# Two order edges in the weight feed of a transformer block: accumulating transfers in source order, copies of sums beside the casts

## The chip, the cores and the metric

The kernel runs on one core of a Trainium2 chip. The metric is device time in microseconds of one execution; a smaller number is better. The kernel before the change was timed three times: 3212.99 us in the median, from 3210.16 to 3214.57. One further execution was recorded by the hardware profiler; it took 3207.22 us, of which 3205.1 us lie between its first and its last instruction (the span).

Engines by the names of the profile: PE is TensorE (matmuls), PEld its weight loads, DVE is VectorE, ACT is ScalarE, POOL is GpSimd, SP is SyncE, which only issues transfers here.

## The reference

Two blocks run one after the other on 512 tokens of width 1024, all in float32. The first is an attention and gated-linear-attention block with a convolutional feed-forward part. The second has four layers; each layer is a mixer and then a multilayer perceptron, and only the perceptrons matter for this change:

```
def _sqrelu_mlp(h, w1, w2):
    return jnp.square(jax.nn.relu(h @ w1)) @ w2
...
    for i in range(DEPTH_2):                       # 4 layers
        ...
        x = x + mix
        x = x + _sqrelu_mlp(_rmsnorm(x, norm_mlp_g[i]), mlp_w1[i], mlp_w2[i])
```

`w1` is 1024 x 4096 and `w2` is 4096 x 1024.

## The kernel before

Activations lie with channels on the 128 partitions and the 512 tokens along the free dimension. Full float32 accuracy is had from three matmuls in a rounded format: each operand is split into a high part (a rounding cast) and a low part (the operand minus its high part), and high x high, high x low and low x high are summed in PSUM. So each weight panel that comes from memory goes through a cast on ScalarE (`split`, line 273, tile `whi`) and a subtraction on VectorE (line 279, tile `wlo`) before TensorE can use it.

A perceptron (`mlp`) runs in four quarters of the 4096 hidden channels. In each quarter the first product (`w1`) takes eight panels of 1024 columns, 192 matmuls of 512 tokens at lines 196 to 198. VectorE scales the result into `H` (line 1171), ScalarE squares it (line 1172), and `quad` forms seven sums and differences of its quadrants and splits them into `hh` and `hl`. The second product (`w2`) is done by a 2 x 2 block scheme with seven products in place of eight: `pair` (line 308) handles two output tiles at a time, four pairs to a quarter, and each of the seven products of a pair is 12 matmuls of 256 tokens at line 327. So the second stage of a quarter has 4 x 7 x 12 = 336 matmuls, and there are 16 such stages in the four perceptrons. Three PSUM banks serve a pair. Most products accumulate on a bank whose partial sum VectorE must first have added to, or subtracted from, the residual `x` (line 1182, `put`), so a later product on the same bank waits for that instruction.

The seven weight operands of a pair are not all plain pieces of `w2`. With a11, a12, a21, a22 as the quadrants, the feed (class `Feed`) makes sums in SBUF with transfers that add to what lies there:

- `raw` holds a11 and a12 and is loaded by SP.
- `s1` = a21 + a22 and `s3` = a11 + a21: SP loads the first term (line 107), and an adding transfer on GpSimd's queue brings the second (line 104).
- `s2` = s1 + a11 and `s4` = s2 + a12: ScalarE copies the older sum into a new tile (line 112), and an adding transfer brings the other term. So each of these copies waits until the adding transfer of the older sum has landed.
- `a22` is loaded by SP.

Each of these steps has a lead: how many half panels ahead of its pair it stands in the source. A half panel is one `split` of 512 columns; two of them fill one `whi` and one `wlo` tile, of which there are three each (`hl_bufs`). The table in the code:

```
    LEAD = {"raw": 4, "s1": 17, "s1+": 14, "s2": 8, "s3": 9, "s3+": 6, "s4": 2, "a22": 3}
```

The order of the source is not the order on the engines. A scheduler places each engine's instructions by its own estimate of when their inputs are there, and only a dependence keeps two instructions in order. `after(first, then)` (class `K`) states such a dependence without a semaphore: the second instruction must stand behind the first on their engine. Before the change nothing of the kind ties the copies of line 112 to the casts of line 273, or one adding transfer of line 104 to another. Each engine takes its instructions in the order in which they stand.

Of the kernel before, what the change touches and what calls it, by code (L numbers as in the profile page):

```python
# [11 lines left out]
ALU = mybir.AluOpType  # L12
# [45 lines left out]
class Feed:  # L58
# [9 lines left out]
    def __init__(self, k, pool, items):  # L68
        self.k, self.pool = k, pool
        self.acts, self.src = [], []  # L70
        self.n, self.at, self.last = 0, 0, 0
        self.tiles, self.got = {}, []
        for i, it in enumerate(items):
            n = len(self.src)
            (self.panel if it[0] == "panel" else self.pair)(i, n, *it)
        self.acts.sort(key=lambda a: a[0])
        self.acts.reverse()
# [16 lines left out]
    def pair(self, i, n, kind, a, b):  # L94

        k, nc = self.k, self.k.nc
        a11, a12, a21, a22 = a[:, :512], a[:, 512:], b[:, :512], b[:, 512:]

        def tile(tag):
            t = self.tiles[i, tag] = self.pool.tile([P, 512], F32, tag=tag, name=k.nm(tag), bufs=self.BUFS[tag])  # L100
            return t

        def add(t, x):
            nc.gpsimd.dma_start(t, x, accum_op=ALU.add)  # L104

        def two(tag, x, y):
            self.act(n, tag, lambda: nc.sync.dma_start(tile(tag), x))
            self.act(n, tag + "+", lambda: add(self.tiles[i, tag], y))

        def more(tag, old, y):  # L110
            t = tile(tag)
            nc.scalar.copy(t, self.tiles[i, old])  # L112
            add(t, y)

        order = self.ORDER[kind]
        where = {"1": ("raw", 0), "2": ("raw", 512), "6": ("s2", 0), "5": ("s1", 0), "7": ("s3", 0), "3": ("s4", 0),
                 "4": ("a22", 0)}
        self.raw(n, i, a)
        two("s1", a21, a22)
        self.act(n, "s2", lambda: more("s2", "s1", a11))  # L120
        two("s3", a11, a21)
        self.act(n, "s4", lambda: more("s4", "s2", a12))
        self.act(n, "a22", lambda: nc.sync.dma_start(tile("a22"), a22))
        self.src += [(i, *where[p]) for p in order]

    def pump(self):
        k = self.k
        while True:
            while self.acts and self.acts[-1][0] <= self.n:
                self.acts.pop()[1]()  # L130
            if self.n == len(self.src) or self.n // 2 - k.hl_bufs >= self.at // 2:
                return
            if self.n % 2 == 0:
                self.pairs = [k.wp.tile([P, PANEL], F32R, tag=t, name=k.nm(t), bufs=k.hl_bufs) for t in ("whi", "wlo")]
            i, tag, c = self.src[self.n]
            h = slice(512 * (self.n % 2), 512 * (self.n % 2) + 512)
            hi, lo = [t[:, h] for t in self.pairs]
            k.split(hi, lo, self.tiles[i, tag][:, c:c + 512])
            self.got.append((hi, lo))
            self.n += 1  # L140

# [8 lines left out]
class K:  # L150
# [119 lines left out]
    def split(self, hi, lo, src, hi_eng="act", lo_eng="dve"):  # L270
        nc = self.nc
        if hi_eng == "act":
            nc.scalar.copy(hi, src)  # L273
        elif hi_eng == "dve":
            nc.vector.tensor_copy(hi, src)
        else:
            nc.gpsimd.tensor_copy(hi, src)
        e = nc.vector if lo_eng == "dve" else nc.gpsimd
        e.tensor_tensor(lo, src, hi.bitcast(F32), ALU.subtract)  # L279

    def sq_add(self, acc, k, last, src, pool, n, scale=1.0, eng=None, apart=False):

        nc = self.nc
        if k == 0:
            nc.scalar.activation(acc, src, AF.Square, scale=scale)
            return
        s = pool.tile([P, n], F32, tag="sq", name=self.nm("sq"), bufs=2)
        nc.scalar.activation(s, src, AF.Square, scale=scale)  # L288
        if k == last and apart:
            return s  # L290
        (nc.vector if k == last else eng or nc.gpsimd).tensor_tensor(acc, acc, s, ALU.add)  # L291
# [1496 lines left out]
```

## Time and profile before

| what | value |
|---|---|
| three timed runs, median (lowest to highest) | 3212.99 us (3210.16 to 3214.57) |
| profiled execution | 3207.22 us |
| its span | 3205.1 us |
| PE busy in the span | 3029.7 us, 95% |
| DVE busy | 2156.5 us, 67% |
| ACT busy | 1488.9 us, 46% |
| POOL busy | 508.7 us, 16% |
| mean granted TensorE clock | 0.974 of full speed |

"Busy" is the time in which at least one instruction of an engine runs. A matmul's end is modelled and matmuls overlap, so the distance between two starts tells the pace better than the duration of one. The waits of an engine are idle stretches before an instruction, put down to what ended last among the things it waited for. The granted clock is the share of TensorE's full speed that the chip allowed; 1.00 is 2.4 GHz and 0.50 is 1.2 GHz.

### The profile page before, as it was taken

Reading aid. Unit: us, or ns where it says so; the run is one execution under the profiler, and the core shown is the slowest. Engines: PE = TensorE matmul, PEld = TensorE weight load, DVE = VectorE, ACT = ScalarE, POOL = GpSimd, SP = SyncE. Lnnn points to the kernel's source line nnn. Section 1 sums busy time; section 2 is a strip of 40 time slices with the busy share of each in tenths; the row PEclk is TensorE's granted clock in tenths of the full one; section 3 lists DMA queues with packets and bytes.
Section 4 is the critical chain, followed back from the end, with each engine's and each line's share of the span. In section 5 each row is a group of like instructions: output and inputs, shape, how many; then the busy total and the mean of one; then the engine's idle time right before and its main releaser. Section 6 shows DMA issues by size and latency. Waiting matters only on the chain.

```text
span 3205.1 us, 42688 instructions
## 1 busy us (share of the span) xinstructions
PE 3029.7 (95%) x16044; PEld 2596.4 (81%) x16044; DVE 2156.5 (67%) x3596; ACT 1488.9 (46%) x2429; POOL 508.7 (16%) x453
## 2 busy tenths in 40 slices
PE   7999999899999998999999999999999999999998
PEld 4877778688887778888887888888888887788887
DVE  7858885599836856666655666754666688665666
ACT  5436644333334744444444444522544457554444
POOL 3103211100012121111102111101211121121111
PEclk8999999899999999999999999999999999999999
DMA  5661234333333346555425666432655644265663
GB/s 195 204 222 52 90 111 154 139 101 97 96 97 109 106 131 161 143 145 142 120 86 143 150 158 155 106 99 99 160 145 150 158 106 139 86 169 141 151 158 86
DMA packets 164271, 421.09 MB, mean 131 GB/s; under 512 B 18240, under 2 KB 24768, under 8 KB 163040
## 3 DMA queue, kind: packets, MB, share of 16 engines
q1 hardware_dynamic: 118000, 334.91, 32.2%
q0 software_dynamic: 36864, 67.13, 13.3%
q10 hardware_dynamic: 9200, 16.32, 1.5%
q8 instruction: 126, 2.06, 0.3%
q14 instruction: 81, 0.66, 0.1%
HBM read 398.10 MB, written 13.63 MB: 128 GB/s over the span
## 4 chain that ended last, share of the span: by engine, by line
PE 59%; DVE 11%; DMA 11%; issue 4%; ACT 4%; POOL 1%; SPq 0%; POOLq 0%; DVEq 0%; ACTq 0%
PE ps L196 15%; PE ps L198 15%; PE ps L197 15%; PE ps L327 10%; DMA s<-in_w 10%; DVE wlo L279 3%; DVE wlo L182 1%; DVE xc L1257 1%; ACT s L112 1%; DVE hl L279 1%; DVE x L1182 1%; ACT whi L273 1%; ACT hh L273 1%; PE po L217 1%; DVE H L1171 0%
## 5 line engine op out<-in xcount | busy, mean ns | idle before, releaser
L196 PE MATMUL ps<-xh,whi 128*128 128x512 f32 x2224 | 872.5, 394 | 10.4 <-ACT xh L501 6.3
L198 PE MATMUL ps<-xh,wlo 128*128 128x512 f32 x2224 | 872.7, 393 | 6.1 <-DVE wlo L182 4.6
L197 PE MATMUL ps<-xl,whi 128*128 128x512 f32 x2224 | 871.5, 392 | 2.8 <-DVE xl L506 2.8
L327 PE MATMUL ps<-hh,whi 128*128 128x256 f32 x1792 | 525.3, 295 | 89.0 <-DVE x L1182 74.2
L327 PE MATMUL ps<-hl,whi 128*128 128x256 f32 x1792 | 521.9, 292 | 2.2 <-DVE hl L279 1.5
L180 ACT CAST whi<-wraw 128x1024 fp32r<-128x1024 f32 (+2 forms) x267 | 265.1, 995 | 552.0 <-PE ps L197 394.0
L327 PE MATMUL ps<-hh,wlo 128*128 128x256 f32 x1792 | 516.6, 290 | 0.0
L198 PEld LDWEIGHTS ps<-xh,wlo 128*128 128x128 f32 x2224 | 420.2, 189 | 98.3 <-DVE wlo L182 7.9
L196 PEld LDWEIGHTS ps<-xh,whi 128*128 128x128 f32 x2224 | 420.6, 189 | 97.7 <-ACT xh L501 6.5
L197 PEld LDWEIGHTS ps<-xl,whi 128*128 128x128 f32 x2224 | 420.4, 189 | 88.9 <-DVE xl L506 3.5
L327 PEld LDWEIGHTS ps<-hh,whi 128*128 128x128 f32 x1792 | 356.4, 200 | 101.0 <-ACT whi L273 70.7
L182 DVE TENSOR_TENSOR wlo<-wraw,whi 128x1024 fp32r<-128x1024 f32 (+2 forms) x257 | 300.0, 1167 | 189.2 <-ACT whi L180 183.4
L104 POOL DMA_DIRECT2D s<-in_w x256 | 224.8, 997 | 1162.7 <-DMA s<-in_w 748.5
L273 ACT CAST whi<-wraw 128x512 fp32r<-128x512 f32 (+2 forms) x400 | 229.9, 612 | 296.4 <-PE ps L197 203.7
L327 PEld LDWEIGHTS ps<-hl,whi 128*128 128x128 f32 x1792 | 357.9, 200 | 5.7 <-DVE hl L279 4.9
L327 PEld LDWEIGHTS ps<-hh,wlo 128*128 128x128 f32 x1792 | 356.7, 200 | 0.0
L279 DVE TENSOR_TENSOR wlo<-wraw,whi 128x512 fp32r<-128x512 f32 (+2 forms) x400 | 266.5, 696 | 39.4 <-ACT whi L273 26.2
L1182 DVE TENSOR_TENSOR x<-x,ps 128x256 f32<-128x256 f32 x448 | 182.6, 418 | 142.0 <-PE ps L327 138.4
L273 ACT CAST whi<-s 128x512 fp32r<-128x512 f32 x256 | 150.5, 618 | 139.0 <-PE ps L327 110.7
L1171 DVE SCALAR_TENSOR_TENSOR H<-ps,rb 128x512 f32<-128x512 f32 x128 | 88.0, 690 | 155.3 <-PE ps L198 152.5
L291 POOL TENSOR_TENSOR acc_x<-acc_x,sq 128x512 f32<-128x512 f32 x54 | 80.4, 1490 | 670.0 <-ACT sq L288 669.5
L112 ACT COPY s<-s 128x512 f32<-128x512 f32 x128 | 79.4, 620 | 221.1 <-DMA s<-in_w 170.7
(418 smaller groups left out, 4526.9 us busy)
## 6 DMA issues: line engine op xcount, KB each, us to landing
wraw<-in_w SPq DMA_DIRECT2D x192, 512.0 KB, 4.0
s<-in_w POOLq DMA_DIRECT2D x256, 256.0 KB, 5.3
s<-in_w SPq DMA_DIRECT2D x128, 256.0 KB, 3.9
wraw<-in_w_up SPq DMA_DIRECT2D x44, 512.0 KB, 3.4
wraw<-in_a_w_in SPq DMA_DIRECT2D x40, 512.0 KB, 3.5
wraw<-in_w_ada SPq DMA_DIRECT2D x32, 512.0 KB, 4.3
a<-in_w SPq DMA_DIRECT2D x64, 256.0 KB, 3.7
wraw<-in_w_in SPq DMA_DIRECT2D x29, 512.0 KB, 3.8
```

The lines of the kernel that those rows point to most:

```text
L104: nc.gpsimd.dma_start(t, x, accum_op=ALU.add)
L112: nc.scalar.copy(t, self.tiles[i, old])
L180: nc.scalar.copy(hi[:, :n], raw[:, :n])
L182: e.tensor_tensor(lo[:, :n], raw[:, :n], hi[:, :n].bitcast(F32), ALU.subtract)
L196: mm(out, wh, xh, start=start, stop=False)
L197: mm(out, wh, xl, start=False, stop=False)
L198: mm(out, wl, xh, start=False, stop=stop)
L273: nc.scalar.copy(hi, src)
L279: e.tensor_tensor(lo, src, hi.bitcast(F32), ALU.subtract)
L327: mm = lambda *o, **kw: self.nc.tensor.matmul(*o, skip_group_check=not start, **kw)
L1171: nc.vector.scalar_tensor_tensor(h, ps, 0.0, self.rb, ALU.max, ALU.mult)
L1182: nc.vector.tensor_tensor(x[:, n, :], x[:, n, :], ps, ALU.add if sign > 0 else ALU.subtract)
```

## The change

Two order edges are added, both without a semaphore. In `add`, each adding transfer of a feed is tied behind the one issued before it in the source, so that GpSimd's queue holds them in the order of the source. In `more`, each copy of a sum on ScalarE is tied behind the high-part cast that precedes it in the source; `split` now returns that cast so that it can be named. No instruction is added or taken away on any engine.

```diff
@@ class Feed, __init__
+        self.added, self.cast = None, None
@@ pair
         def add(t, x):
-            nc.gpsimd.dma_start(t, x, accum_op=ALU.add)
+            d = nc.gpsimd.dma_start(t, x, accum_op=ALU.add)
+            if self.added is not None:
+                k.after(self.added, d)
+            self.added = d
...
         def more(tag, old, y):
             t = tile(tag)
-            nc.scalar.copy(t, self.tiles[i, old])
+            c = nc.scalar.copy(t, self.tiles[i, old])
+            if self.cast is not None:
+                k.after(self.cast, c)
             add(t, y)
@@ pump
-            k.split(hi, lo, self.tiles[i, tag][:, c:c + 512])
+            self.cast = k.split(hi, lo, self.tiles[i, tag][:, c:c + 512])
@@ split
-            nc.scalar.copy(hi, src)
+            i = nc.scalar.copy(hi, src)
...
         e.tensor_tensor(lo, src, hi.bitcast(F32), ALU.subtract)
+        return i
```

Lines behind the edits have moved: 104 is now 105, 112 is 116, 273 and 279 are 279 and 285, 1172 is 1179, 1182 is 1189.

The first place is ScalarE in the second stage of the second quarter of the first perceptron, around its third pair of output tiles. `whi1668` to `whi1685` are the high parts in the order in which TensorE uses them; `s21670` is the tile `s2` number 1670, and so on. `s21717` and `s41735` are sums of the next quarter. Before:

```order
L273 CAST whi1668_10718<-s41649_10569 128x512
L273 CAST whi1668_10718<-a221644_10527 128x512
L112 COPY s41679_10826<-s21670_10722 128x512
L273 CAST whi1671_10753<-wraw1659_10648 128x512 x2
L273 CAST whi1673_10786<-s21651_10576 128x512
L273 CAST whi1673_10786<-s11622_10387 128x512
L112 COPY s21717_11124<-s11696_10967 128x512
L273 CAST whi1677_10822<-s31650_10572 128x512
L273 CAST whi1677_10822<-s41663_10684 128x512
L112 COPY s41735_11259<-s21717_11124 128x512
L273 CAST whi1683_10860<-a221662_10680 128x512
```

The same stretch with the change:

```order
L279 CAST whi1668_10718<-s41649_10569 128x512
L116 COPY s21670_10722<-s11645_10529 128x512
L279 CAST whi1668_10718<-a221644_10527 128x512
L279 CAST whi1671_10753<-wraw1659_10648 128x512 x2
L279 CAST whi1673_10786<-s21651_10576 128x512
L279 CAST whi1673_10786<-s11622_10387 128x512
L279 CAST whi1677_10822<-s31650_10572 128x512
L116 COPY s41679_10826<-s21670_10722 128x512
L279 CAST whi1677_10822<-s41663_10684 128x512
L279 CAST whi1683_10860<-a221662_10680 128x512
```

The two copies for the next quarter have left this stage (they now stand in the first stage of the next quarter, among the casts of `w1`), and the copies of the fourth pair's own sums (`s21670`, `s41679`) stand later, each between the two casts of one panel.

The second place is GpSimd's queue in the same stage, with the adding transfers alone. Before:

```order
L104 DMA s41649_10569<-in_w2 128x512
L104 DMA s11645_10529<-in_w2 128x512
L104 DMA s21651_10576<-in_w2 128x512
L104 DMA s41663_10684<-in_w2 128x512
L104 DMA s31650_10572<-in_w2 128x512
L104 DMA s21670_10722<-in_w2 128x512
L104 DMA s11696_10967<-in_w2 128x512
L104 DMA s41679_10826<-in_w2 128x512
L104 DMA s31664_10687<-in_w2 128x512
L104 DMA s21717_11124<-in_w2 128x512
```

With the change:

```order
L105 DMA s41649_10569<-in_w2 128x512
L105 DMA s21651_10576<-in_w2 128x512
L105 DMA s11645_10529<-in_w2 128x512
L105 DMA s31650_10572<-in_w2 128x512
L105 DMA s41663_10684<-in_w2 128x512
L105 DMA s21670_10722<-in_w2 128x512
L105 DMA s31664_10687<-in_w2 128x512
L105 DMA s41679_10826<-in_w2 128x512
L105 DMA s11696_10967<-in_w2 128x512
L105 DMA s21717_11124<-in_w2 128x512
```

The transfer of `s11696`, which belongs to the next quarter, now stands behind the two of the fourth pair, and that of `s11645` behind that of `s21651`, which needs a copy first.

The third place is VectorE around the third pair, where the low parts (`wlo`) and the additions to the residual (`x`) share the engine. Before:

```order
L279 TENSOR_TENSOR wlo1678_10823<-s31650_10572,whi1677_10822 128x512
L279 TENSOR_TENSOR wlo1678_10823<-s41663_10684,whi1677_10822 128x512
L1182 TENSOR_TENSOR x_4888<-x_4888,ps1680_10831 128x256
L1182 TENSOR_TENSOR x_4888<-x_4888,ps1681_10832 128x256
L279 TENSOR_TENSOR wlo1684_10861<-a221662_10680,whi1683_10860 128x512
```

With the change:

```order
L285 TENSOR_TENSOR wlo1678_10823<-s31650_10572,whi1677_10822 128x512
L1189 TENSOR_TENSOR x_4888<-x_4888,ps1680_10831 128x256
L285 TENSOR_TENSOR wlo1678_10823<-s41663_10684,whi1677_10822 128x512
L1189 TENSOR_TENSOR x_4888<-x_4888,ps1681_10832 128x256
L285 TENSOR_TENSOR wlo1684_10861<-a221662_10680,whi1683_10860 128x512
```

The addition from `ps1680` now stands ahead of the second low part, whose cast comes after a copy on ScalarE. The other stages change in the same way, and SyncE's order does not change at all. In the last quarter of a perceptron no next quarter exists, so only the copies of its own pairs move there.

## Rows read from the trace of the kernel before

**Rows 1.** The page: busy time, then the chain that ended last by line.
```profile
PE 3029.7 (95%) x16044; PEld 2596.4 (81%) x16044; DVE 2156.5 (67%) x3596; ACT 1488.9 (46%) x2429; POOL 508.7 (16%) x453
...
PE ps L196 15%; PE ps L198 15%; PE ps L197 15%; PE ps L327 10%; DMA s<-in_w 10%; DVE wlo L279 3%; DVE wlo L182 1%; DVE xc L1257 1%; ACT s L112 1%; DVE hl L279 1%; DVE x L1182 1%; ACT whi L273 1%; ACT hh L273 1%; PE po L217 1%; DVE H L1171 0%
```

**Rows 2.** Waits of TensorE: who waited for whom, total us, times, longest.
```profile
PE ps L327 <- DVE x L1182: 74.2, 42, 5.6
PE ps L327 <- ACT hh L273: 14.7, 4, 4.5
```

**Rows 3.** Windows of line 327, quarters one to three: stretch, length, PE, PEld, clock, DMA.
```profile
1332.60:1381.00 48.40, 43.63 (x336) 42.72 (x335) 0.93 0.77 171
...
sum 608.20, PE 528.08 PEld 515.91; mean PE 44.01 PEld 42.99
```

**Rows 4.** Windows of the four last quarters, all engines: PE, PEld, DVE, ACT, POOL.
```profile
1517.60:1563.10 45.50, 42.08 (x338) 40.83 (x337) 39.09 (x65) 26.54 (x45) 12.23 (x10) 1.00 0.45 105
...
sum 179.00, PE 167.68 PEld 162.98 DVE 149.59 ACT 100.57 POOL 47.85; mean PE 41.92 PEld 40.74 DVE 37.40 ACT 25.14 POOL 11.96
```

**Rows 5.** Windows, the first stage (w1) of the second quarter, all engines.
```profile
1289.30:1332.50 43.20, 43.20 (x192) 35.78 (x191) 27.02 (x51) 20.86 (x38) 1.73 (x2) 1.00 0.43 123
```

**Rows 6.** Timeline of TensorE, two starts that are twelve matmuls apart: start, duration.
```profile
1376.04 0.28 PE L327 MATMUL ps<-hh,wlo 128*128 128x256 f32 x1
...
1377.48 0.28 PE L327 MATMUL ps<-hh,wlo 128*128 128x256 f32 x1
```

**Rows 7.** Timeline of ScalarE, second quarter, second stage: start, duration, [idle before].
```profile
1337.17 0.83 ACT L273 CAST hh<-qt 128x768 fp32r<-128x768 f32 x1 [1.09 <-DVE qt L303]
...
1345.07 0.62 ACT L273 CAST whi<-s 128x512 fp32r<-128x512 f32 x1 [1.55 <-PE ps L327]
1345.60 0.62 ACT L273 CAST whi<-a 128x512 fp32r<-128x512 f32 x1
...
1350.83 1.14 ACT L273 CAST whi<-s 128x512 fp32r<-128x512 f32 x2 [1.49 <-PE ps L327]
...
1353.71 1.14 ACT L273 CAST whi<-s 128x512 fp32r<-128x512 f32 x2 [0.33 <-PE ps L327]
1361.19 0.62 ACT L112 COPY s<-s 128x512 f32<-128x512 f32 x1 [6.34 <-DMA s<-in_w]
```

**Rows 8.** Timeline of VectorE, the same stretch.
```profile
1362.36 0.69 DVE L279 TENSOR_TENSOR wlo<-a,whi 128x512 fp32r<-128x512 f32 x1 [5.22 <-ACT whi L273]
...
1363.57 0.74 DVE L1182 TENSOR_TENSOR x<-x,ps 128x256 f32<-128x256 f32 x2
```

**Rows 9.** Timeline of TensorE, the same stretch.
```profile
1364.13 0.55 PE L327 MATMUL ps<-hh,whi 128*128 128x256 f32 x1 [4.58 <-DVE x L1182]
```

**Rows 10.** Windows, the stretch behind that wait, all engines.
```profile
1363.60:1369.00 5.40, 4.87 (x23) 4.90 (x24) 2.34 (x6) 0.90 (x2) 1.13 (x2) 0.50 0.90 183
```

**Rows 11.** Timeline of GpSimd: the adding transfers of `s11645` and `s21717`.
```profile
1327.08 0.86 POOL L104 DMA_DIRECT2D s<-in_w  x1 [40.51 <-DMA s<-in_w]
...
1353.69 0.86 POOL L104 DMA_DIRECT2D s<-in_w  x1 [2.55 <-ACT s L112]
```

**Rows 12.** Landing times of the adding transfers: whole run, then issues 1348.4 to 1352.
```profile
DMA to landing us min/median/max: 4.1/5.3/11.2
...
DMA to landing us min/median/max: 4.2/8.2/9.7
```

**Rows 13.** Timeline of ScalarE, then of TensorE, first quarter, first pair.
```profile
1241.97 0.62 ACT L112 COPY s<-s 128x512 f32<-128x512 f32 x1 [3.06 <-DMA s<-in_w]
...
1243.16 0.58 PE L327 MATMUL ps<-hh,whi 128*128 128x256 f32 x1 [3.78 <-ACT hh L273]
```

**Rows 14.** Waits of TensorE from 1332.6 to 1359.0, all there are.
```profile
PE ps L327 <- DVE x L1182: 0.2, 1, 0.2
```

**Rows 15.** Waits of ScalarE over the span, the one of the copies.
```profile
ACT s L112 <- DMA s<-in_w: 170.7, 58, 9.1
```

More of the change, by code (lines that the diff above doesn't have):

```diff
@@ L272, in split @@
         if hi_eng == "act":
-            nc.scalar.copy(hi, src)
+            i = nc.scalar.copy(hi, src)
         elif hi_eng == "dve":
-            nc.vector.tensor_copy(hi, src)
+            i = nc.vector.tensor_copy(hi, src)
         else:
-            nc.gpsimd.tensor_copy(hi, src)
+            i = nc.gpsimd.tensor_copy(hi, src)
         e = nc.vector if lo_eng == "dve" else nc.gpsimd
         e.tensor_tensor(lo, src, hi.bitcast(F32), ALU.subtract)
+        return i
     def sq_add(self, acc, k, last, src, pool, n, scale=1.0, eng=None, apart=False):
```

## Prediction

> **What bounds the kernel now.** I read the page first. TensorE is busy 95% of the span, and most of the chain that ended last lies in its lines 196 to 198 and 327; but that chain also holds 10% of waiting for the adding transfers `s<-in_w` [rows 1]. So TensorE is the bound, and the question is where it still stops. The view of waits, for TensorE, answers: one place leads by far. Line 327, the second stage of the perceptrons, waits 74.2 us for VectorE's additions to the residual and 14.7 us for ScalarE's `hh` [rows 2].
>
> The next view is the table by windows, one window for each second stage. The four last quarters take 179.0 us together, 44.75 each [rows 4]; the twelve other stages take 608.2 us, 50.7 each, for the same 336 matmuls [rows 3]. The first stage of a quarter, in contrast, has no idle time: TensorE is busy 43.20 of 43.20 us [rows 5]. Whatever this change does to TensorE it does at line 327.
>
> What would such a stage take without waits? Two starts that are twelve matmuls apart lie 1.44 us apart, so 0.120 us for each [rows 6]; 336 of them are 40.3 us, and with the tail of the last one (0.28 us long) 40.5. So the twelve stages hold 608.2 - 12 x 40.5 = 122 us that are not matmul pace, and the last quarters 179.0 - 4 x 40.5 = 17 us.
>
> Now the cause, in the timelines of one stage, that of 48.4 us [rows 3]. While TensorE paces it, ScalarE casts a panel every 2.88 us: one at 1345.07, the second after it at 1350.83, the third at 1353.71 [rows 7]. The next should come at 1356.6. It doesn't: ahead of its casts stands the copy `s41735`, a sum of the next quarter, and ScalarE idles 6.34 us before it, until 1361.19, for an adding transfer to land [rows 7]. That transfer could go out only at 1353.69, released by the copy of the older sum [rows 11], and so took 7.5 us. VectorE gets its low part at 1362.36, after 5.22 us of idling, and only behind the low parts stands the addition to the residual, at 1363.57 [rows 8]. On that addition waits the next product on the same bank: TensorE starts again at 1364.13, having idled 4.58 us [rows 9].
>
> The stop costs more than itself. In the 5.4 us behind it the granted clock is 0.50, and TensorE starts 23 matmuls [rows 10] where its pace would allow 45: it has fallen to the level of 1.2 GHz because it had stopped. The last quarter of the same perceptron, without a long stop, shows 1.00 throughout [rows 4], this stage 0.93 [rows 3].
>
> The first quarters have a second stop of this kind: the copy `s41551` stands ahead of a split of the squared `H` and waits 3.06 us for its transfer, and TensorE idles 3.78 us for the `hh` behind it [rows 13]. Four such waits are the 14.7 us in the view of waits. Apart from its big stop the stage at 1332.6 loses little: 0.2 us of waits in its first 26 us [rows 14].
>
> **The change part by part.** No instruction is added, so busy times stay; only places move.
>
> *The copies for the next quarter leave the second stage.* In the new order `s21717` and `s41735` stand among the casts of the next first stage, where TensorE needs a new panel only every 5.4 us (43.20 us for eight) and has no waits at all [rows 5]. The transfers that they need go out long before. So the wait of 6.34 us goes in each of the twelve stages, and with it the stop of TensorE and the slow clock behind it. `s41551` and its likes in the first quarters move behind the casts of the next panels, and that stop goes too.
>
> *The copies of a stage's own sums stand later.* What is late next? Two copies could be: `s21670`, now between the two casts of the panel of 1345.07, and `s41679`, between the two of 1353.71. I step through the stage with the times that it had before its stop. `s41679` needs the transfer of `s21670`. That copy takes the place of the second cast at 1345.60, ends 0.62 us later at 1346.2 [rows 7], and its transfer lands 4.1 to 11.2 us after its issue, 5.3 in the median [rows 12]: with an issue at 1346.5 that is 1351.8, at the worst 1357.7. ScalarE reaches `s41679` at 1353.71 + 0.53 = 1354.2. So 2.4 us to spare at the median, and a wait of 3.5 us at the worst. Long landings belong to bunches: the three issued from 1348.4 on landed after 8.2 us in the middle [rows 12], and of these three one is of the next quarter and now stands last.
>
> A wait there also hurts less than the one removed. VectorE's addition from `ps1680` now stands ahead of the second low part, the one that the copy delays, so TensorE's next product on that bank is not held up. I put the tolerance at one product, 1.44 us [rows 6].
>
> *The copies between two casts delay the second cast.* By 0.53 us (1345.07 to 1345.60 is what one cast of the same size takes) [rows 7]. The cover is the lead of the panel, which TensorE needs two panels later; without cover two copies in each of twelve stages cost 12.7 us. Below nothing this can't go, since a copy doesn't speed a cast. No row shows such a copy hidden, so I take the upper end, and with it the 0.2 us of waits of each undisturbed stage [rows 14]: 12.7 + 2.4 = 15 us.
>
> *The adding transfers in source order.* That of `s11645`, issued at 1327.08 before [rows 11], now stands behind that of `s21651`, whose copy stands just ahead of the cast of 1337.17 [rows 7]. So it goes out by 1338.1 (one issue of 0.86 us later) and lands at 1343.4 in the median, at the worst at 1349.3. The copy that needs it comes at 1345.6. Cover 2.2 us; at the worst a wait of 3.7. I cost it at nothing. A rule speaks against this part: the Trainium skill (DMA: Bandwidth & Descriptors, Anatomy of one DMA) says that a transfer's semaphore wait happens on the issuing sequencer before dispatch, so in strict order one that waits for its copy holds back every ready one behind it. By this rule the gain could turn round, which is the third rival. The same page's fit for a transfer from GpSimd (2.0 us and the bytes at 436 GB/s) gives 2.6 us for 256 KB as an estimate, and by it no copy would wait; the trace has 4.1 us at the least, and the sum goes by the trace.
>
> *The last quarters.* VectorE is busy 39.1 of 45.5 us there, and the clock stays at 1.00 [rows 4]: their 17 us are mostly VectorE's queue. Copies and additions trade places there too. By the rows all 17 us could go, or as much again come; I take nothing.
>
> **Sum.** 122 us of excess, less 15 that stay, is 107 us. Against the profiled execution that is 3207 - 107 = 3100. The median of the three runs is 6 us above that execution, so I forecast 3213 - 107 = 3106, and write 3107.
>
> **The rivals.**
>
> *Half of it comes back as shorter waits.* If landings take 10 to 11.2 us even unbunched, both mid-panel copies of a stage wait 2.3 to 3.7 us; less the tolerance, TensorE loses 0.9 to 2.3 us at each, 1.6 in the middle. For it: the DMA engines are 0.77 busy in this stage [rows 3]. Against it: fewer transfers in the stage, and a median of 5.3 us. Two such waits in 16 stages are 50 us: 3157.
>
> *Nothing moves.* The transfers might be the true limit, and a later copy would only wait elsewhere for the same landing. For it: the 10% in the chain [rows 1]. Against it: ScalarE's copies wait 170.7 us in all [rows 15], and the longest one seen here is for a sum that no cast needs before the next quarter's second stage. 3213. That the order stays as it is can be left out: the new rows show it.
>
> *Slower: GpSimd's queue holds back what is ready.* If `s11645`'s transfer lands only behind 1351.6, ScalarE stops between two casts for 6 us; less the tolerance TensorE stops 4.6, as at 1364, and its slow clock follows (half of the 5.4 us): 7.3 us in each of 16 stages, 117, on top of 3107: 3224. It decides from a landing 13.5 us after the issue; the largest in the trace is 11.2 [rows 12].
>
> **How the numbers follow.** The forecast has 0.80 (3090 to 3130, by the bounds of the mid-panel copies and the last quarters). Half comes back: 0.12. Nothing moves: 0.03. Slower: 0.05. A measurement of this kernel tells about 0.2%, 6 us, from no change. So faster 0.92, same 0.03, slower 0.05. The range, 3090 to 3155, takes in the forecast and most of the first rival.
>
> **What would show it.** Right: in the second stages of quarters one to three the granted clock reads 1.00 and each takes 41 to 43 us; line 327's wait for VectorE falls from 74.2 us to below 20 and its wait for `hh` to near nothing; ScalarE's copies wait below 40 us in place of 170.7. Wrong at the copies: a wait of ScalarE of more than 2 us before a copy between two casts of one panel. Wrong in the transfers: a ready transfer of GpSimd behind one that waits for its copy, and then a copy that waits for its landing. The forecast falls if these stages still show a clock below 1.00, or if the first stages begin to idle because the copies went there.

## The result and the profile after

The changed kernel took 3079.63 us in the median of three runs (3076.32 to 3083.64), against 3212.99 before: a ratio of 0.9587, with a 95% interval from 0.9565 to 0.9609. The forecast was 3107, with a range from 3090 to 3155. So the direction and the place were right, and the gain was larger than forecast by 27 us, past the faster end of the range.

The profiled execution of the changed kernel is the one of 3079.63 us; its span is 3077.8. First its page: busy time, and the chain that ended last.

```profile
PE 2989.1 (97%) x16044; PEld 2566.1 (83%) x16044; DVE 2159.4 (70%) x3596; ACT 1475.9 (48%) x2429; POOL 508.8 (17%) x453
...
PE ps L334 20%; PE ps L202 18%; PE ps L204 18%; PE ps L203 18%; DVE wlo L188 1%; DVE xc L1264 1%; PE po L223 1%; DVE wlo L285 1%; PE pu L928 0%; DVE xc L1338 0%; PE pt L811 0%; DVE tg L1336 0%; PE ps L223 0%; ACT whi L186 0%; DVE x L1189 0%
```

Against [rows 1], the 10% of waiting for adding transfers has left the chain, and line 334 (327 before) holds 20% in place of 10%: where the chain ran through that waiting, it now runs through matmuls. The view of waits says the same (who waited for whom, total us, times, longest):

```profile
POOL s L105 <- ACT s L116: 513.5, 87, 24.8
...
ACT s L116 <- DMA s<-in_w: 11.2, 6, 4.1
...
PE ps L334 <- DVE x L1189: 5.1, 9, 1.0
```

TensorE's wait for the additions to the residual fell from 74.2 to 5.1 us, its wait for `hh` is gone [rows 2], and the copies on ScalarE wait 11.2 us for transfers in place of 170.7 [rows 15]. The waits of GpSimd for these copies grew from 244.8 to 513.5 us; TensorE's waits show no cost of that.

The windows of line 334, quarters one to three, answer to [rows 3]; one is shown, and the sum of twelve.

```profile
1320.20:1361.00 40.80, 40.75 (x336) 40.38 (x335) 1.00 0.74 182
...
sum 489.50, PE 489.19 PEld 484.89; mean PE 40.77 PEld 40.41
```

The same for all engines: a first stage (as [rows 5]), and the last quarters (as [rows 4]).

```profile
1276.90:1320.10 43.20, 43.20 (x192) 35.77 (x191) 27.16 (x51) 21.42 (x40) 6.15 (x7) 1.00 0.60 145
...
1488.50:1531.90 43.40, 41.70 (x338) 40.88 (x337) 37.98 (x65) 27.26 (x47) 14.58 (x13) 1.00 0.54 122
...
sum 171.20, PE 166.13 PEld 163.08 DVE 144.72 ACT 103.72 POOL 57.78; mean PE 41.53 PEld 40.77 DVE 36.18 ACT 25.93 POOL 14.45
```

The twelve stages take 40.8 us each, at a clock of 1.00: 608.2 - 489.5 = 118.7 us gained. The first stage still has no idle time, although copies went there. The four last quarters took 179.0 and take 171.2: 7.8 us more. Together that is 126.5 of the 127.3 us between the two spans.

The timeline of ScalarE around the third pair of the second quarter shows the copies in their new places, at 1332.60 (`s21670`) and 1341.23 (`s41679`), each between the two casts of a panel:

```profile
1332.07 0.62 ACT L279 CAST whi<-s 128x512 fp32r<-128x512 f32 x1 [1.03 <-PE ps L334]
1332.60 0.62 ACT L116 COPY s<-s 128x512 f32<-128x512 f32 x1
1333.12 0.61 ACT L279 CAST whi<-a 128x512 fp32r<-128x512 f32 x1
1334.95 1.14 ACT L279 CAST whi<-wraw 128x512 fp32r<-128x512 f32 x2 [1.22 <-PE ps L334]
1337.83 1.14 ACT L279 CAST whi<-s 128x512 fp32r<-128x512 f32 x2 [1.74 <-PE ps L334]
1340.71 0.62 ACT L279 CAST whi<-s 128x512 fp32r<-128x512 f32 x1 [1.74 <-PE ps L334]
1341.23 0.62 ACT L116 COPY s<-s 128x512 f32<-128x512 f32 x1
```

ScalarE idles 1.74 us ahead of a pair of casts without a copy and 1.22 us ahead of the pair that follows a copy: the 0.52 us between them is the copy, paid out of idle time. Neither copy waits. For the second it is close: the adding transfer of `s21670` was issued at 1333.51 and took 7.7 us, so it landed at 1341.2. In three of the twelve stages this copy did wait, 0.80, 0.31 and 0.22 us, and they too took 40.8 us; the other 9.9 of the 11.2 us lie in first stages, where no wait of TensorE stands beside them. The landing times over the whole run, then of this transfer:

```profile
DMA to landing us min/median/max: 4.1/6.5/10.4
...
DMA to landing us min/median/max: 7.7/7.7/7.7
```

### The profile page after: what moved, and what is told of

Same layout as the page of the kernel before. It is cut to its first block, busy times and chain, and to the rows that moved or that the text cites. A ratio compares the mean times of both kernels' runs of the same rounds, so it can differ in the third digit from the quotient of the medians.

```text
span 3077.8 us, 42669 instructions
## 1 busy us (share of the span) xinstructions
PE 2989.1 (97%) x16044; PEld 2566.1 (83%) x16044; DVE 2159.4 (70%) x3596; ACT 1475.9 (48%) x2429; POOL 508.8 (17%) x453
## 4 chain that ended last, share of the span: by engine, by line
PE 78%; DVE 7%; ACT 2%; issue 2%; POOL 1%; DMA 0%; SPq 0%; POOLq 0%; DVEq 0%; ACTq 0%
PE ps L334 20%; PE ps L202 18%; PE ps L204 18%; PE ps L203 18%; DVE wlo L188 1%; DVE xc L1264 1%; PE po L223 1%; DVE wlo L285 1%; PE pu L928 0%; DVE xc L1338 0%; PE pt L811 0%; DVE tg L1336 0%; PE ps L223 0%; ACT whi L186 0%; DVE x L1189 0%
## 5 line engine op out<-in xcount | busy, mean ns | idle before, releaser
L334 PE MATMUL ps<-hh,whi 128*128 128x256 f32 x1792 | 511.1, 285 | 5.1 <-DVE x L1189 5.1
L334 PE MATMUL ps<-hl,whi 128*128 128x256 f32 x1792 | 508.0, 283 | 0.0
L334 PE MATMUL ps<-hh,wlo 128*128 128x256 f32 x1792 | 504.2, 283 | 0.0
L105 POOL DMA_DIRECT2D s<-in_w x256 | 223.9, 1038 | 1053.2 <-ACT s L116 513.5
L334 PEld LDWEIGHTS ps<-hh,whi 128*128 128x128 f32 x1792 | 343.4, 192 | 10.3 <-ACT whi L279 3.5
L334 PEld LDWEIGHTS ps<-hl,whi 128*128 128x128 f32 x1792 | 343.6, 192 | 0.7
L334 PEld LDWEIGHTS ps<-hh,wlo 128*128 128x128 f32 x1792 | 342.4, 192 | 0.0
L285 DVE TENSOR_TENSOR wlo<-s,whi 128x512 fp32r<-128x512 f32 x256 | 178.9, 715 | 10.4 <-ACT whi L279 1.2
```

The lines of the kernel that those rows point to most:

```text
L105: d = nc.gpsimd.dma_start(t, x, accum_op=ALU.add)
L334: mm = lambda *o, **kw: self.nc.tensor.matmul(*o, skip_group_check=not start, **kw)
```

## The experiments

All start from the changed kernel. "Twelve" are the second stages of quarters one to three together, "last" the four last quarters. Each ratio is to the kernel before as timed beside that kernel (medians of 3204 to 3211 us), so it is not the quotient of two medians of the table.

| kernel | median us | ratio to before (95%) | twelve | last |
|---|---|---|---|---|
| before | 3212.99 | 1 | 608.2 | 179.0 |
| changed | 3079.63 | 0.9587 (0.9565 to 0.9609) | 489.5 | 171.2 |
| adds tied only | 3239.83 | 1.0096 (1.0074 to 1.0118) | 635.6 | 180.6 |
| copies tied only | 3095.93 | 0.9638 (0.9613 to 0.9664) | 489.6 | 181.2 |
| copies made twice | 3099.72 | 0.9653 (0.963 to 0.9676) | 502.6 | 176.5 |
| last quarters untied | 3091.46 | 0.9632 (0.9613 to 0.9652) | 489.5 | 181.0 |
| s4 earlier | 3098.20 | 0.9676 (0.9647 to 0.9706) | 489.3 | 185.5 |
| first pairs' copies only | 3145.94 | 0.9814 (0.9786 to 0.9843) | 541.3 | 189.3 |
| sums of squares on VectorE | 3074.95 | 0.9599 (0.9575 to 0.9623) | 489.6 | 167.7 |
| idle second copy | 3081.67 | 0.9616 (0.9593 to 0.9638) | 491.9 | 169.4 |
| changed, again | 3082.09 | 0.9594 (0.958 to 0.9608) | 489.6 | 171.1 |
| s2 earlier | 3108.81 | 0.9679 (0.9662 to 0.9697) | 499.7 | 173.5 |
| s2 earlier, sums on VectorE | 3107.07 | 0.9673 (0.9659 to 0.9687) | 499.8 | 170.4 |

The work outside these sixteen stages took 2416 to 2426 us from one profiled execution to the next (2431 and 2438 in the two with `s2` earlier), whatever the order in the stages; so a stage sum tells more than a median.

A stop "behind matmul 215" lies between the matmuls 215 and 216 of a second stage, counted from 0 (the expectations say "product 215"). Where no line is shown, its size is the distance of the two starts less the pace of 0.12 us; that is some 0.16 us more than the idle time that a view gives.

### Each edge alone

The transfers' edge alone (the copies' edge taken out):

```diff
-            if self.cast is not None:
-                k.after(self.cast, c)
```

> Only the adding transfers are tied; the copies of sums are free again. ScalarE's and VectorE's queues are then those of before but for about 20 places, and GpSimd's queue is that of the change but for 10. Theory (the gain lies in where the copies stand on ScalarE): nothing of the gain stays, 3213 us, 3200 to 3225; line 334's wait for VectorE near 74 us; the copies' waits for transfers near 170 us; the twelve second stages of quarters one to three near 608 us together. Rival (the transfers' order carries half of the gain, since a sum that is needed soon no longer queues behind one that is needed late): about 3150 us, and the twelve stages near 550.

Both theories fell: alone, this edge makes the kernel slower, by 1%. The sum of its windows, and then its timelines of GpSimd, ScalarE and TensorE in the second quarter:

```profile
sum 635.60, PE 535.31 PEld 519.63; mean PE 44.61 PEld 43.30
```

```profile
1358.32 2.65 POOL L105 DMA_DIRECT2D s<-in_w  x3 [7.62 <-DMA s<-in_w]
...
1368.57 0.62 ACT L116 COPY s<-s 128x512 f32<-128x512 f32 x1 [8.78 <-DMA s<-in_w]
...
1371.52 0.55 PE L332 MATMUL ps<-hh,whi 128*128 128x256 f32 x1 [5.50 <-DVE x L1187]
```

The copy of `s21717`, for the next quarter, still stands in this stage and needs the transfer of `s11696`. In source order that transfer stands behind those of `s31664` and `s41679`; it is the last of the three that go out from 1358.32, at 1359.39. So ScalarE stops 8.78 us ahead of casts that are due, and TensorE 5.50 us. Before, it went out ahead of them. This is the mechanism of the third rival, at another tile than it named.

The copies' edge alone (the transfers' edge taken out):

```diff
-            if self.added is not None:
-                k.after(self.added, d)
-            self.added = d
```

> Only the copies of sums are tied; the adding transfers are free again. ScalarE's and VectorE's queues are then exactly those of the change, GpSimd's differs in 142 of 458 places. Theory (copies are the gain): 3080 us, 3075 to 3090, the twelve stages 40.8 each. Rival (the order of the transfers is needed too: the copy of s41679 has 0.04 us to spare in the changed kernel, so one transfer of the next quarter ahead of its own, 0.86 us of issue and up to 3 us of later landing, makes ScalarE wait between two casts): 1 to 2.5 us in each of the twelve stages, 3092 to 3110.

ScalarE's and VectorE's queues are those of the changed kernel, and so are the twelve stages. The copies' places are therefore the whole gain there, as the theory had it; but its 3080 was too low, since the last quarters lose 10.0 us. The rival's 3092 to 3110 held 3095.93, but its waits in the twelve stages did not come. First its windows, the twelve and the last; then its timelines in the last quarter of the second perceptron:

```profile
sum 489.60, PE 489.29 PEld 484.91; mean PE 40.77 PEld 40.41
...
sum 181.20, PE 169.48 PEld 166.63 DVE 145.11 ACT 103.79 POOL 54.34; mean PE 42.37 PEld 41.66 DVE 36.28 ACT 25.95 POOL 13.59
```

```profile
1994.93 0.62 ACT L113 COPY s<-s 128x512 f32<-128x512 f32 x1
...
1998.43 1.78 POOL L105 DMA_DIRECT2D s<-in_w  x2 [2.38 <-DVE wlo L282]
...
2007.50 0.62 ACT L113 COPY s<-s 128x512 f32<-128x512 f32 x1 [4.60 <-DMA s<-in_w]
...
2009.84 0.55 PE L331 MATMUL ps<-hh,whi 128*128 128x256 f32 x1 [4.64 <-ACT xh L1107]
```

The copy of `s22501` was done at 1995.55, but its transfer stood behind that of `s32494`, which waited for VectorE until 1998.43; it went out as the second of this pair, at 1999.01. That is 4.08 us after its copy started; in the changed kernel, where `s22501` goes first by source order, it is 1.07 (1983.80 to 1984.87), so 3.0 us of delay come from the order. The landing grew too, from 4.7 us to 8.5 beside the other transfer of the pair. The next copy waits 4.60 us for it, and TensorE stops. (The view names `xh`, but that instruction ended at 2002.09; what ended last ahead of 2009.84 is VectorE's addition, from 2009.28, behind the low part of the delayed cast.)

The Trainium skill (DMA: Bandwidth & Descriptors, Anatomy of one DMA) says that a transfer's semaphore wait happens on the issuing sequencer, before dispatch. Both runs agree: a transfer that waits delays the ones behind it in its queue, here by 3.0 us. So the transfers' edge pays in the last quarters, and only beside the copies' edge: alone it left them at 180.6 us.

### Which copies matter

Adds tied, and of the copies only those for the first pair of a quarter:

```diff
-            if self.cast is not None:
+            if self.cast is not None and kind == "late":
```

> Adding transfers tied as in the change; of the copies only those for the first pair of a quarter are tied (the two that stood in the second stage of the quarter before). Theory (these two are the whole of the big stop at product 215): it is gone in all twelve stages; the first quarters keep their stop of 3 to 4.5 us at product 32, where a copy still stands ahead of a split of the squared H, and the last quarters stay near 179 us: twelve stages near 525 together, 3120 us. Rival (transfers in strict order and free copies of the stage's own sums block one another, as in the run with adds alone, where product 191 stopped for 5.3 us): stops of 3 to 5 us stay in each stage, twelve stages near 580, 3175 us.

The big stop behind matmul 215 is gone in all twelve stages, but they fall only to 541.3: 66.9 of the 118.7 us. Against the transfers' edge alone, the kernel that differs by these copies only, it is 94.3 us (635.6 to 541.3), and 51.8 remain. The rest belongs to the copies of the stage's own sums, the only further ones that the changed kernel ties. Stops behind matmul 143 (0.6 to 3.0 us) stay in nine of the stages, and in three of the four first quarters the large one behind matmul 32, 3.4 to 5.2 us, here in the first perceptron:

```profile
1244.52 0.58 PE L334 MATMUL ps<-hh,whi 128*128 128x256 f32 x1 [5.04 <-ACT hh L279]
```

The theory was right on the place and 16 us too low on the sum; the rival's stops behind matmul 191 did not come. Both had the last quarters near 179 us; they took 189.3, and in three of the four the stop behind matmul 143 is 2.0 to 3.8 us, against 1.1 to 1.6 before.

### What a copy between two casts costs

Each copy made twice, both needed by its transfer:

```diff
-            c = nc.scalar.copy(t, self.tiles[i, old])
-            if self.cast is not None:
-                k.after(self.cast, c)
+            for _ in range(2):
+                c = nc.scalar.copy(t, self.tiles[i, old])
+                if self.cast is not None:
+                    k.after(self.cast, c)
```

> Both edges, and each copy of a sum is made twice, into the same tile and at the same place: 112 more ScalarE copies of 0.53 to 0.62 us. My prediction's step (a copy between two casts costs TensorE what it takes, 0.53 us, twice in each of twelve stages): plus 12.7 us, 3092 us, and the twelve stages 41.9 each. Rival (the lead of the panels hides a copy, the 15 us of the prediction were too dear): within 3 us of the changed kernel, 3080, the twelve stages 40.8 to 41.0, although the next transfer goes out 0.53 us later and the copies of s4 wait for its landing.

502.6 for the twelve stages, 13.1 us more, looks like my step (12.7). The timelines of ScalarE and TensorE say otherwise:

```profile
1252.39 0.62 ACT L117 COPY s<-s 128x512 f32<-128x512 f32 x1 [1.82 <-DMA s<-in_w]
1252.92 0.61 ACT L280 CAST whi<-a 128x512 fp32r<-128x512 f32 x1
...
1254.73 0.36 PE L335 MATMUL ps<-hh,whi 128*128 128x256 f32 x1 [0.99 <-DVE x L1190]
```

The copy of `s21558` waits 1.82 us, since the transfers go out later. At this place the second copy does not even stand between the two casts: the scheduler put it behind them, at 1253.44. In the second quarter the copy at this place waits 0.11 us, and that stage takes 40.8 us with all its copies doubled. To part the two causes, the next kernel makes the second copy into a tile that nobody reads, behind the first, so that the transfer needs only the first:

```diff
             add(t, y)
+            if self.scr is None:
+                self.scr = self.pool.tile([P, 512], F32, tag="scr", name=k.nm("scr"), bufs=1)
+            k.after(c, nc.scalar.copy(self.scr, self.tiles[i, old]))
```

> Both edges, and behind each copy of a sum a second copy of the same tile goes to a tile that nobody reads; the adding transfer needs only the first, so it goes out no later. ScalarE's own time alone is doubled: 0.53 us twice between casts in each second stage. My prediction's step (that time reaches TensorE): the twelve stages 41.9 each, plus 12.7 us, 3092. Rival (the lead of the panels hides ScalarE's time, and the 13 us of the run with doubled copies came from transfers that went out later and landed too late): 40.8 to 41.0 each, 3080.

```profile
sum 491.90, PE 490.68 PEld 484.64; mean PE 40.89 PEld 40.39
```

Here both copies stand between the two casts (1334.34 and 1334.87, with the second cast at 1335.38). It costs 2.4 us, where ScalarE's time alone would have made 12.7: most of a copy's time doesn't reach TensorE. Eight of the twelve stages take 40.8 us; the other four take 0.2 to 1.2 us more. In its timeline of ScalarE, a wait that was hidden and one that was not quite:

```profile
1334.34 0.62 ACT L116 COPY s<-s 128x512 f32<-128x512 f32 x1 [0.39 <-DMA s<-in_w]
...
1419.31 0.62 ACT L116 COPY s<-s 128x512 f32<-128x512 f32 x1 [1.16 <-DMA s<-in_w]
```

Waits at this place up to 0.50 us cost nothing, and those of 0.88, 1.16 and 1.77 us stopped TensorE for 0.13, 0.41 and 1.01: the wait, less 0.75. These three stops are 1.6 of the 2.4 us.

### How much later a transfer may land

The step that makes `s4` stands two half panels earlier:

```diff
-    LEAD = {"raw": 4, "s1": 17, "s1+": 14, "s2": 8, "s3": 9, "s3+": 6, "s4": 2, "a22": 3}
+    LEAD = {"raw": 4, "s1": 17, "s1+": 14, "s2": 8, "s3": 9, "s3+": 6, "s4": 4, "a22": 3}
```

> Both edges, and the step that makes s4 stands four half panels ahead of its pair in the source in place of two. The copy of s41567 and its likes then stand one panel earlier (2.88 us, between the two casts of the panel before), where the adding transfer of s2 has not landed: by the times of the changed kernel each waits 2.1 to 3.0 us. Theory (what counts is the landing: TensorE stops for the wait less about 0.65 us, as the waits of 1.3 to 2.0 us did in the run with doubled copies): 1.5 to 2.3 us at one product of each of twelve stages, 18 to 28 us and somewhat more where the clock falls: 3100 to 3115 us, the twelve stages 42.3 to 43.5. Rival (the lead of two panels covers a wait of 3 us): 3080, 40.8.

The rival was right for the twelve stages, 489.3. The copies waited 0.2 to 1.3 us there, less than I had worked out, and all of it was hidden. In the last quarters waits of 2.0 to 2.6 us stopped TensorE for 2.8 to 3.9, more than the wait: behind it VectorE had low parts and `xl` to do, up to 1.75 us each, ahead of the addition. A hidden and an open one, in the timelines of ScalarE and TensorE:

```profile
1340.21 0.62 ACT L116 COPY s<-s 128x512 f32<-128x512 f32 x1 [1.14 <-DMA s<-in_w]
...
1510.03 0.62 ACT L116 COPY s<-s 128x512 f32<-128x512 f32 x1 [2.58 <-DMA s<-in_w]
...
1516.96 0.58 PE L334 MATMUL ps<-hh,whi 128*128 128x256 f32 x1 [3.77 <-DVE x L1189]
```

The other direction gives the transfer more time, with `s2` two half panels earlier. It was timed beside the changed kernel:

```diff
-    LEAD = {"raw": 4, "s1": 17, "s1+": 14, "s2": 8, "s3": 9, "s3+": 6, "s4": 2, "a22": 3}
+    LEAD = {"raw": 4, "s1": 17, "s1+": 14, "s2": 10, "s3": 9, "s3+": 6, "s4": 2, "a22": 3}
```

> The changed kernel once more, beside the two that follow. Theory (the gain sits in the order alone): the twelve stages 489.6 us together and the last quarters 171.2, as in its first profile, and the same small waits of the copies; 3075 to 3085 us. Rival (landings differ from execution to execution, and a margin of 0.04 us was luck): waits of 1 to 3 us at s41679 in some stages, 495 us or more.

> Both edges, and the step that makes s2 stands ten half panels ahead of its pair in place of eight, so that its transfer has 2.9 us more before the copy of s4 comes. Theory (no copy waits where it matters): no change in the twelve stages, 489.6, and at most 1 us less in the last quarters: 3080 us. Rival (an earlier copy of s2 meets the transfer of s1 that it needs, in strict order on GpSimd's queue): waits of 1 to 3 us move there, 3085 to 3100.

The changed kernel came out as in its first profile. In one stage two earlier copies did wait, 0.77 and 0.60 us, and the stage took 40.8 all the same. With the three waits of the first profile, this says that the margin of some 0.04 us was small, but not what held the gain. With `s2` earlier it is slower, and in the sixteen stages by neither of my two stories. Every one of them now stops for 0.85 us behind matmul 35. First VectorE's timeline of the changed kernel, then that of this one with TensorE's below it:

```profile
1324.05 0.41 DVE L1189 TENSOR_TENSOR x<-x,ps 128x256 f32<-128x256 f32 x1
1324.38 0.95 DVE L285 TENSOR_TENSOR hl<-qt,hh 128x768 fp32r<-128x768 f32 x1
```

```profile
1326.21 0.95 DVE L285 TENSOR_TENSOR hl<-qt,hh 128x768 fp32r<-128x768 f32 x1
1327.08 1.07 DVE L1189 TENSOR_TENSOR x<-x,ps 128x256 f32<-128x256 f32 x3
...
1327.54 0.50 PE L334 MATMUL ps<-hh,whi 128*128 128x256 f32 x2 [0.69 <-ACT whi L279]
```

The scheduler put the first addition to the residual behind the split of 0.95 us that it stood ahead of, and TensorE starts again at 1327.54, as the first of the three additions ends. (The view names a cast that ended at the same time, 1327.49; it is the first half panel of the next pair, behind `a22`, which this matmul does not read.)

A further 11 us lie in the first stage of the first quarter of the third and the fourth perceptron, and there the rival was right in kind. Copies of `s2` wait 6.11 and 5.22 us for the sum that they copy, against 4.20 and 2.77 in the changed kernel, and what stands behind them has changed: on ScalarE the copy is now ahead of `rmsw`, a step of the norm that TensorE needs. In the changed kernel, run again, `rmsw` stood ahead of it (2200.35, the copy at 2205.27), and TensorE had no such wait. ScalarE's timeline, then TensorE's, with `s2` earlier:

```profile
2209.19 0.62 ACT L116 COPY s<-s 128x512 f32<-128x512 f32 x1 [6.11 <-DMA s<-in_w]
2209.72 0.20 ACT L243 ACTIVATE rmsw<-rmsw 128x4 f32<-128x4 f32 x1
...
2212.25 1.10 PE L264 MATMUL ps<-rmsd,ones_r 128*128 128x512 f32 x2 [3.22 <-DVE rmsd L260]
```

VectorE idles 5.70 us for `rmsw`, TensorE 3.22 us for the `rmsd` made from it, and from 2212 to 2218 the granted clock is 0.72, where that first stage of the changed kernel shows 1.00. From the first matmul of the stage to the last it is 50.2 us in place of 44.7; in the fourth perceptron it is 50.6 in place of 44.7. That is the mechanism which the change removes elsewhere, brought back by a constant.

### The last quarters

The last three pairs of each fourth quarter set free again:

```diff
+        self.free = len(items) - 3
...
-            if self.added is not None:
-                k.after(self.added, d)
-            self.added = d
+            if i < self.free:
+                if self.added is not None:
+                    k.after(self.added, d)
+                self.added = d
...
-            if self.cast is not None:
+            if self.cast is not None and i < self.free:
```

> Both edges, but not for the last three pairs of the fourth quarter of each perceptron: copies and transfers of these are free again. Theory A (the 7.9 us that the four last quarters gained come from their own order): they go back from 171.2 to 179 us together and the kernel to 3088. Theory B (they come from what the feed no longer carries over from the quarters before): they stay at 171 to 173, the kernel at 3080 to 3082. The twelve other stages stay at 489.6 by both.

Theory A: 181.0 with the twelve at 489.5. The gain there is made by the quarter's own order. Where VectorE was slow before, it still is; but the addition that TensorE needs behind matmul 197 now stands ahead. VectorE's timeline of before, then of the changed kernel with GpSimd's below it:

```profile
1542.91 1.75 DVE L1104 SCALAR_TENSOR_TENSOR xl<-x,vecs,xh 128x512 fp32r<-128x512 f32 x1
1544.59 0.41 DVE L1182 TENSOR_TENSOR x<-x,ps 128x256 f32<-128x256 f32 x1
```

```profile
1511.85 0.41 DVE L1189 TENSOR_TENSOR x<-x,ps 128x256 f32<-128x256 f32 x1
1512.39 1.34 DVE L1111 SCALAR_TENSOR_TENSOR xl<-x,vecs,xh 128x512 fp32r<-128x512 f32 x1
...
1513.98 1.45 DVE L285 TENSOR_TENSOR wlo<-a,whi 128x512 fp32r<-128x512 f32 x1
1515.36 0.68 DVE L285 TENSOR_TENSOR wlo<-wraw,whi 128x512 fp32r<-128x512 f32 x1
...
1511.89 2.99 POOL L298 TENSOR_TENSOR acc_x<-acc_x,sq 128x512 f32<-128x512 f32 x2
```

The `xl` and the low part beside GpSimd's `acc_x` take 1.34 and 1.45 us, the one behind them 0.68. In this quarter the stop behind matmul 197 fell from 0.98 us to nothing. It is not the only one that moved: the stop behind matmul 143 fell from 1.51 to 0.36, where two low parts beside GpSimd's addition had taken 2.68 us and now, apart from it, take 1.28, and the one behind matmul 215 grew from 0.47 to 1.16. So the additions of `acc_x` were given to VectorE:

```diff
-        self.sq_last = self.sq_add(self.acc, m, KD - 1, xm, pool, T, apart=last)
+        self.sq_last = self.sq_add(self.acc, m, KD - 1, xm, pool, T, eng=nc.vector, apart=last)
```

> Both edges, and the running sums of squares in the residual step (eight a last quarter, and those of the other blocks) run on VectorE in place of GpSimd. Theory A (the stops of 0.36, 1.16 and 0.65 us that the last quarters keep come from VectorE's operations that take 1.3 to 1.8 us in place of 0.69 while GpSimd adds): they go, the last quarters fall from 171.2 to 164 to 167 together, 3075 us. Theory B (VectorE is too full there: eight additions of 0.69 us are 5.5 us more in each): the stops grow, 175 to 181, 3085 us or more.

```profile
1511.23 0.74 DVE L1111 SCALAR_TENSOR_TENSOR xl<-x,vecs,xh 128x512 fp32r<-128x512 f32 x1
1511.89 0.69 DVE L298 TENSOR_TENSOR acc_x<-acc_x,sq 128x512 f32<-128x512 f32 x1
1512.50 0.41 DVE L1189 TENSOR_TENSOR x<-x,ps 128x256 f32<-128x256 f32 x1
1512.83 0.69 DVE L285 TENSOR_TENSOR wlo<-a,whi 128x512 fp32r<-128x512 f32 x1
```

Theory A on the mechanism: with more to do, VectorE is done sooner, since `xl` takes 0.74 us and the low part 0.69 again. The last quarters fall to 167.7, a little above the 164 to 167 expected, by 3.5 us or 0.1%. That is below what a median tells here: the ratios to before overlap. With `s2` earlier as well:

> The running sums of squares on VectorE and s2 ten half panels ahead, both edges kept. Theory: the gains add: last quarters 167 to 168 us together as with the sums alone, twelve stages 489.6: 3075 us, 0.1 to 0.2% below the changed kernel. Rival: the earlier copies of s2 disturb the last quarters, 172 or more, and it is no better than the changed kernel.

The gains do not add: the stop behind matmul 35 comes along (499.8 us for the twelve stages), the last quarters take 170.4, below the rival's 172, and the kernel is slower. No version measurably better than the changed kernel was found.

## Why the prediction was off

**Right: the bound, the place and the pace.** Line 327 was where TensorE stopped, 40.5 us was the time of a stage without waits (40.8 measured), and the waits that were to fall fell. "Half comes back" and "nothing moves" are refuted by 11.2 us of copy waits.

**Wrong: "the copies between two casts delay the second cast", 12.7 us, and 2.4 beside it.** This is the step that failed. Of these 15 us, 3.5 stay (489.5 - 12 x 40.5), and no run shows that even these are the copies'. I took the upper end because no row showed a copy hidden. [Rows 7] held the answer: ScalarE sat idle 1.49 to 1.55 us ahead of a pair of casts, waiting for TensorE to free a panel, and a copy of 0.53 us fits in there twice. The idle second copy shows it: the copies' time between the casts doubled, and 2.4 us were lost, most of them to late landings.

**Wrong: "the last quarters: nothing".** They gained 7.8 us. The untied run shows that they gain it by their own order, and the runs with one edge alone (180.6 and 181.2 us) that it takes both. My bounds, 17 us either way, held it.

**An offset.** I took the gain from the profiled execution, 3207.22 us, and set it off from the median, 5.8 us above it. The work outside the stages varies by as much. So of 27.4 us, 11.7 are the copies, 7.8 the last quarters, 5.8 the offset, and 2.1 rounding and the rest of the span. The copies alone would have left 3095, inside the range; it took a second term to leave it.

**Right by luck: "2.4 us to spare".** The transfer took 7.7 us, not 5.3, and about 0.04 were left; in three stages nothing was. Nor is the tolerance of one product, 1.44 us, shown: at the copy of `s2` (`s21558` and its likes) it was 0.75. At the copy of `s4`, where I had put it, the longest wait of any run was 1.01 us (sums of squares on VectorE) and its stage took 40.8, so its end was not reached.

**The adding transfers at nothing: right in sum, wrong in kind.** In the twelve stages they add nothing once the copies are placed, and cost 27.4 us alone (635.6 - 608.2). I gave the mechanism 0.05 for the whole change. It is real, and needs a copy that is wanted late standing in front of casts that are wanted now; the copies' edge removes just that.

What stays open: why that transfer took 7.7 us. No run took the DMA load away.

## What to carry to other kernels

Where one engine both feeds the bound engine and prepares work for later, an instruction for later whose input may be late must not stand ahead of the feed; where only a scheduler's guess decides, tie it. Tie the queue that delivers its input only together with it: an order edge that makes a transfer late is harmless only if nobody waits for it at the wrong place. And before pricing an inserted instruction by its duration, look for the idle time in front of its neighbours: if the engine waits there for buffers, the instruction is free, and what counts is when its result lands.

## What the runs showed that I had not expected

VectorE operations of 0.69 to 0.75 us took 1.3 to 1.8 us beside a GpSimd addition, so that moving that addition to the busier engine shortened the stage (171.2 to 167.7 for four). And two changes of one constant in a table of leads, meant to touch transfers alone, made a copy wait or moved an addition on VectorE, and cost 14.1 us (`s4` earlier) and 12.5 us (`s2` earlier) in the sixteen stages, the second another 11 us ahead of them.
